# Softmax minus one-hot: stores move to Pool as single DMA packets and wait for a load four rows ahead

## The chip, the core and the metric

The kernel runs on one core of a Trainium2 chip. The core has compute engines that work side by side (VectorE, called DVE in the profile; ScalarE, called ACT; GpSimd, called POOL; TensorE, called PE) and SyncE (SP), which here only issues DMAs. All DMAs of the core, whichever engine issues them, are carried out by the same 16 DMA engines. The metric is the device time of one execution in microseconds; the kernel before was run three times: 1248.03 us in the median, 1247.41 to 1248.87.

## The reference

Input are logits of 8 x 1024 x 8192 float32 and one integer label for each of the 8192 rows. The output is the gradient of softmax cross entropy, as large as the logits:

```python
logits_max = np.max(logits, axis=-1, keepdims=True)
exp_logits = np.exp(logits - logits_max)
softmax = exp_logits / np.sum(exp_logits, axis=-1, keepdims=True)
...
one_hot[batch_idx, seq_idx, labels] = 1.0
return (softmax - one_hot).astype(np.float32)
```

So 268.4 MB are read and 268.4 MB are written, and each element is touched a few times in between.

## The kernel before

The 8192 rows of logits are cut into 32 blocks of 256 rows. In a block, partition p of the 128 holds two neighbouring rows, j = 0 and j = 1. The kernel's unit of work, which it calls a row and numbers t = 0 to 63, is one j of one block: 128 partitions with 8192 float32 each, 32 KB a partition, 4 MB in all. Block b is t = 2b and 2b + 1. The large tile `X` holds three blocks (`SLOTS = 3`), so six rows: all that is loaded, computed on in place and not yet stored has to fit in these six places.

For each row t there are these instructions. VectorE finds the negated maximum (`m<-X`, the tensor reduce). ScalarE computes exp(x + m) in place and sums it (`X<-X,m`). VectorE takes the reciprocal of the sum (`r<-s`). ScalarE scales the row by it (`X<-X,r`). VectorE compares a constant row of column numbers (`iota`, in PSUM) with the label and subtracts the resulting one-hot (`X<-iota,lab,X`). The last row is scaled and subtracted in two halves. Ahead of all that, Pool, TensorE and VectorE prepare the column numbers and turn the labels; this borrows the sixth place of `X`, which is why the load of row 5 waits for `w_iota`.

All instructions are issued by a helper `run` (lines 63 to 74), which gives them their semaphore waits; that is why nearly every instruction has line 68 in the profile, and a wait that stands in front of one has line 67. The order on each engine is the order in which the code is written. On VectorE it is: reciprocal of row t, maximum of row t + 1, subtraction of row t.

Loads are issued by SP (`nc.sync`, `load(b)`), on one DMA queue, which is q1 in the profile. The string `LOADS` says how each block is loaded: "r" as two DMAs, one for each row; "w" as one DMA for both rows, so 64 KB contiguous for a partition. Blocks 0 to 4 and 26 to 31 are "r", blocks 5 to 25 are "w". A load waits until the stores of the same place three blocks earlier have landed (`free`).

Stores are issued by ACT (`nc.scalar`, `store(t)`), one DMA for each row, on another queue, which is q10. The store of row t - 1 is written in ACT's order between the exp and the scaling of row t, so it is issued as soon as row t - 1 is finished and ACT comes to it.

Of the kernel before, what the change touches and what calls it, by code (L numbers as in the profile page):

```python
# [7 lines left out]
P = 128  # L8
G = 2
SLOTS = 3  # L10


LOADS = "rrrrrwwwwwwwwwwwwwwwwwwwwwrrrrrr"
STORES = "rrrrrrrrrrrrrrrrrrrrrrrrrrrrrrrr"


@with_exitstack
def kernel(
    ctx: ExitStack,
    tc: tile.TileContext,  # L20
    logits: bass.AP,
    labels: bass.AP,
    out: bass.AP,
):
    nc = tc.nc
    fp32 = mybir.dt.float32
    i32 = mybir.dt.int32
    i16 = mybir.dt.int16
    Act = mybir.ActivationFunctionType
    Alu = mybir.AluOpType  # L30

    x_nv = logits.flatten_outer_dims()
    o_nv = out.flatten_outer_dims()
    N, V = x_nv.shape
    T = N // P
    B = T // G
    lab_bp = labels.rearrange("a b -> (a b)").rearrange("(b q) -> b q", q=G * P)
    x_b = x_nv.rearrange("(b p j) v -> b p j v", p=P, j=G)
    o_b = o_nv.rearrange("(b p j) v -> b p j v", p=P, j=G)

    const = ctx.enter_context(tc.tile_pool(name="const", bufs=1))
    psum = ctx.enter_context(tc.tile_pool(name="psum", bufs=1, space=bass.MemoryType.PSUM))


    X = const.tile([P, SLOTS, G, V], fp32)
    lab_raw = const.tile([B, G * P], labels.dtype)
    lab_f = const.tile([B, G, P], fp32)
    ident = const.tile([B, B], fp32)
    lab = const.tile([P, G, B], fp32)

    m, s, r = (const.tile([P, T], fp32, name=n) for n in ("m", "s", "r"))

    iota = psum.tile([P, V], i16)
    lab_ps = iota[:].bitcast(fp32)[:, :T].rearrange("p (j b) -> p j b", j=G)

    with tc.tile_critical():  # L56
        sem = tc.alloc_semaphore
        got = [[sem(f"got{i}{q}") for q in range(2)] for i in range(SLOTS)]
        put = [[sem(f"put{i}{q}") for q in range(2)] for i in range(SLOTS)]
        lab_got, dve, act, pe, pool = (sem(n) for n in ("lab_got", "dve", "act", "pe", "pool"))  # L60
        count = {}

        def run(engine, waits, counter, method, **operands):

            waits = list(dict.fromkeys(waits))
            for w in waits[:-1]:
                engine.wait_ge(*w)
            instruction = getattr(engine, method)(**operands)  # L68
            for w in waits[-1:]:
                instruction._wait_ge(*w)  # L70
            step = 16 if method == "dma_start" else 1
            instruction.then_inc(counter, step)
            count[counter.name] = count.get(counter.name, 0) + step
            return counter, count[counter.name]


        w_raw = run(nc.scalar, [], lab_got, "dma_start", out=lab_raw[:], in_=lab_bp)
        w = run(nc.gpsimd, [], pool, "memset", ap=ident[:], constant=0.0)
        w_ident = run(
            nc.gpsimd, [w], pool, "affine_select",  # L80
            out=ident[:], in_=ident[:], compare_op=Alu.not_equal, fill=1.0,
            base=0, pattern=[[-1, B]], channel_multiplier=1,
        )

        made = X[:, SLOTS - 1, G - 1, :].bitcast(i16)[:, :V]
        w_made = run(
            nc.gpsimd, [], pool, "iota", out=made, pattern=[[1, V]], base=0, channel_multiplier=0
        )
        step = mybir.dt.size(labels.dtype) // 4
        lab32 = lab_raw[:].bitcast(i32).rearrange("b (p j s) -> b j p s", j=G, s=step)  # L90
        w_lab = run(nc.vector, [w_raw], dve, "tensor_copy", out=lab_f[:], in_=lab32[:, :, :, 0])
        for j in range(G):
            w = run(
                nc.tensor, [w_ident, w_lab], pe, "transpose",
                out=lab_ps[:, j, :], in_=lab_f[:, j, :], identity=ident[:],
            )
        w_turned = run(nc.vector, [w], dve, "tensor_copy", out=lab[:], in_=lab_ps)
        w_iota = run(
            nc.vector, [w_turned, w_made], dve, "tensor_scalar",
            out=iota[:].bitcast(i32), in0=made.bitcast(i32), scalar1=0, scalar2=None, op0=Alu.bitwise_or,  # L100
        )


        every, rows = slice(0, P), slice(0, G)
        PIECES = {
            "r": [(every, slice(j, j + 1)) for j in range(G)],
            "h": [(slice(i, P, 2), rows) for i in range(2)],
            "w": [(every, rows)],
        }

        def meets(a, b):

            sets = [[set(range(*d.indices(n))) for d, n in zip(p, (P, G))] for p in (a, b)]
            return all(x & y for x, y in zip(*sets))


        loaded, stored, finished = {}, {}, []
        last_made = [((every, slice(G - 1, G)), w_iota)]

        def load(b):  # L120
            loaded[b] = []
            before = stored.get(b - SLOTS, last_made if b == SLOTS - 1 else [])
            for q, piece in enumerate(PIECES[LOADS[b]]):
                ps, js = piece
                free = [w for other, w in before if meets(piece, other)]
                w = run(
                    nc.sync, free, got[b % SLOTS][q], "dma_start",
                    out=X[ps, b % SLOTS, js, :], in_=x_b[b, ps, js, :],
                )
                loaded[b].append((piece, w))  # L130

        def store(t):
            b, j = divmod(t, G)
            stored.setdefault(b, [])
            for q, piece in enumerate(PIECES[STORES[b]]):
                ps, js = piece
                if js.stop != j + 1:
                    continue
                w = run(
                    nc.scalar, [finished[t]], put[b % SLOTS][q], "dma_start",  # L140
                    out=o_b[b, ps, js, :], in_=X[ps, b % SLOTS, js, :],
                )
                stored[b].append((piece, w))


        def row(t):
            return X[:, t // G % SLOTS, t % G, :]

        def row_max(t):
            b, j = divmod(t, G)  # L150
            arrived = [w for piece, w in loaded[b] if meets(piece, (every, slice(j, j + 1)))]
            return run(
                nc.vector, arrived, dve, "tensor_reduce",
                out=m[:, t : t + 1], in_=row(t), axis=mybir.AxisListType.X, op=Alu.max, negate=True,
            )


        load(0)
        w_max = row_max(0)
        for t in range(T):  # L160
            x = row(t)
            label = lab[:, t % G, t // G : t // G + 1]
            w = run(
                nc.scalar, [w_max], act, "activation",
                out=x, in_=x, func=Act.Exp, bias=m[:, t : t + 1], scale=1.0, accum_out=s[:, t : t + 1],
            )
            w_sum = run(nc.vector, [w], dve, "reciprocal", out=r[:, t : t + 1], in_=s[:, t : t + 1])
            if t + 1 < T:
                if (t + 1) % G == 0:
                    load((t + 1) // G)  # L170
                w_max = row_max(t + 1)
            if t > 0:
                store(t - 1)

            n = 1 if t + 1 < T else 2
            cols = [slice(i * V // n, (i + 1) * V // n) for i in range(n)]
            scaled = [
                run(
                    nc.scalar, [w_sum], act, "activation",
                    out=x[:, c], in_=x[:, c], func=Act.Copy, bias=0.0, scale=r[:, t : t + 1],  # L180
                )
                for c in cols
            ]
            for c, w in zip(cols, scaled):
                w = run(
                    nc.vector, [w], dve, "scalar_tensor_tensor",
                    out=x[:, c], in0=iota[:, c], scalar=label, in1=x[:, c],
                    op0=Alu.is_equal, op1=Alu.subtract, reverse1=True,
                )
            finished.append(w)  # L190
        store(T - 1)
        for b in range(B - SLOTS, B):
            for _, w in stored[b]:
                nc.scalar.wait_ge(*w)


# [28 lines left out]
```

## Time and profile before

| | |
|---|---|
| time of the runs, median (lowest to highest) | 1248.03 us (1247.41 to 1248.87) |
| span of the profiled execution | 1245.7 us |
| VectorE busy | 1119.2 us, 90% |
| ScalarE busy | 919.1 us, 74% |
| Pool busy | 7.4 us, 1% |
| DMA packets, bytes, mean rate | 15460, 536.98 MB, 431 GB/s |
| from issue to landing: stores, row loads, block loads (median) | 30.8, 26.6, 33.4 us |

The profiled execution's own time is its span, from the first to the last instruction; the time of a run holds a little more around it, so the median is 2.3 us above the span. The tensor reduce takes 8.68 us a row, the exp 7.12, the scaling 7.12 and the subtraction of the one-hot 8.74. Beside the page, the trace holds a record of each DMA packet (its queue, bytes, begin and duration) and of each landing; a packet here is what one DMA engine moves for one descriptor, for example 32 KB of one partition. In the packet records and everywhere else times are counted from the span's start.

### The profile page before, as it was taken

How to read it: one execution, taken by the hardware profiler on the slowest of the kernel's cores; microseconds unless marked ns; L12 is line 12 of the kernel's file. 1: busy time of each engine (PE TensorE's matmuls, PEld its weight loads, DVE VectorE, ACT ScalarE, POOL GpSimd, SP SyncE). 2: the span in 40 equal slices, each digit the busy share in tenths (PEclk: the TensorE clock that was granted, in tenths of full speed). 3: DMA queues.
4: the chain of work that ended last, by engine and by line, in shares of the span. 5: the costliest groups of instructions: out<-in, count | busy, mean ns of one | idle time of the engine just before them, and what ended most of it. 6: DMA issues, size and time to landing. Idle time of an engine off the chain costs nothing.

```text
span 1245.7 us, 592 instructions
## 1 busy us (share of the span) xinstructions
PE 0.4 (0%) x2; PEld 0.3 (0%) x2; DVE 1119.2 (90%) x196; ACT 919.1 (74%) x194; POOL 7.4 (1%) x7
## 2 busy tenths in 40 slices
PE   0000000000000000000000000000000000000000
PEld 0000000000000000000000000000000000000000
DVE  5999998888988889888998888988889999999893
ACT  3888886778776787767877778777777788887772
POOL 2000000000000000000000000000000000000000
DMA  9999999999999999999999999999999999999998
GB/s 406 417 429 433 438 433 442 437 426 427 430 435 445 439 417 442 426 430 437 432 443 438 420 435 432 430 437 450 420 426 437 436 428 432 437 435 429 432 437 386
DMA packets 15460, 536.98 MB, mean 431 GB/s; under 512 B 1728, under 2 KB 1728, under 8 KB 1760
## 3 DMA queue, kind: packets, MB, share of 16 engines
q1 hardware_dynamic: 6192, 268.44, 50.0%
q10 hardware_dynamic: 9264, 268.51, 49.9%
q14 instruction: 4, 0.03, 0.0%
HBM read 268.50 MB, written 268.44 MB: 431 GB/s over the span
## 4 chain that ended last, share of the span: by engine, by line
DMA 59%; DVE 37%; another core or an unknown queue 2%; ACT 1%; DVEq 0%; issue 0%; PE 0%; SPq 0%; ACTq 0%
DMA X<-in_logits_dram 31%; DMA out_dram<-X 27%; DVE m L68 18%; DVE X L68 18%; ACT X L68 1%; DVE iota L68 0%; DVEq L56 0%; DMA lab_raw<-in_labels_dram 0%; DVE lab_f L68 0%; DVE r L68 0%; PE iota L68 0%; SPq L68 0%; ACTq L68 0%; DVE lab L68 0%
## 5 line engine op out<-in xcount | busy, mean ns | idle before, releaser
L68 DVE TENSOR_REDUCE m<-X 128x1 f32<-128x8192 f32 x64 | 555.2, 8675 | 94.3 <-DMA X<-in_logits_dram 94.3
L68 ACT ACTIVATE X<-X,m 128x8192 f32<-128x8192 f32 x64 | 455.9, 7123 | 188.4 <-DVE m L68 188.4
L68 DVE SCALAR_TENSOR_TENSOR X<-iota,lab,X 128x8192 f32<-128x8192 int16 (+1 forms) x65 | 559.7, 8612 | 4.1 <-ACT X L68 4.1
L68 ACT ACTIVATE X<-X,r 128x8192 f32<-128x8192 f32 (+1 forms) x65 | 456.0, 7017 | 115.9 <-DVE r L68 115.9
L68 DVE RECIPROCAL r<-s 128x1 f32<-128x1 f32 x64 | 9.9, 154 | 7.3 <-ACT X L68 7.3
L68 ACT ACTIVATION_READ_ACCUMULATOR X<-X,m 128x1 f32 x64 | 12.0, 187 | 0.0
L68 DVE CAST lab_f<-lab_raw 32x256 f32<-32x256 int32 x1 | 3.7, 3685 | 4.7 <-DMA lab_raw<-in_labels_dram 4.7
L68 POOL IOTA X<- 128x8192 int16 x1 | 6.9, 6944 | 0.0
L68 DVE TENSOR_SCALAR iota<-X 128x4096 int32<-128x4096 int32 x1 | 4.4, 4427 | 0.1
L68 ACT ACT_TABLE_LOAD x1 | 1.3, 1283 | 1.3 <-SPq L56 1.3
L68 DVE COPY lab<-iota 128x64 f32<-128x64 f32 x1 | 0.2, 225 | 0.5 <-PE iota L68 0.5
L68 PE MATMUL iota<-ident,lab_f 32*128 32x32 f32 x2 | 0.4, 300 | 8.5 <-DVE lab_f L68 8.5
L68 PEld LDWEIGHTS iota<-ident,lab_f 32*128 32x128 f32 x2 | 0.3, 196 | 8.4 <-DVE lab_f L68 8.4
L68 POOL TENSOR_SCALAR_AFFINE_SELECT ident<-ident 32x32 f32<-32x32 f32 x1 | 0.2, 204 | 0.1
L68 POOL MEMSET ident<- 32x32 f32 x1 | 0.1, 115 | 0.5 <-SPq L56 0.5
L209 POOL MEMSET const-bfloat16-1.0<- 128x1 bf16 x1 | 0.1, 107 | 0.0
L209 POOL MEMSET const-uint8-127<- 128x1 uint8 x1 | 0.1, 107 | 0.0
L209 POOL MEMSET const-float32-0.0<- 128x1 f32 x1 | 0.1, 104 | 0.2 <-issue 0.2
L209 POOL MEMSET const-float32-1.0<- 128x1 f32 x1 | 0.1, 104 | 0.0
## 6 DMA issues: line engine op xcount, KB each, us to landing
out_dram<-X ACTq DMA_DIRECT2D x64, 4096.0 KB, 30.8
X<-in_logits_dram SPq DMA_DIRECT2D x22, 4096.0 KB, 26.6
X<-in_logits_dram SPq DMA_DIRECT2D x21, 33.4
lab_raw<-in_labels_dram ACTq DMA_DIRECT2D x1, 64.0 KB, 3.8
```

The costliest lines, as they stand in the source:

```text
L68: instruction = getattr(engine, method)(**operands)
L209: nc = _bacc.Bacc("TRN2", target_bir_lowering=False, num_devices=1)
```

## The change

Loads go row by row for all 64 rows: `load(t)` replaces `load(b)`, the strings `LOADS` and `STORES` and the table `PIECES` go away, and a load of row t waits for the store of row t - 6 alone. Stores are issued by Pool (`nc.gpsimd`) instead of ACT, with `single_packet=True`, which asks for one DMA packet for each engine instead of one for each descriptor; each engine's share of a row's store is 8 partitions, 256 KB. The store of row t additionally waits until the load of row t + 4 has landed (`AHEAD = 4`); the last four stores, and so those of rows 60 to 63, have no such wait of their own. A store is written in Pool's order once the load it waits for has been written. The closing waits for the last six stores are Pool's.

```diff
-LOADS = "rrrrrwwwwwwwwwwwwwwwwwwwwwrrrrrr"
-STORES = "rrrrrrrrrrrrrrrrrrrrrrrrrrrrrrrr"
+AHEAD = 4
...
+        loaded, stored, finished, stores = {}, {}, [], []
+
+        def load(t):
+            b, j = divmod(t, G)
+            free = w_iota if t == SLOTS * G - 1 else stored[t - SLOTS * G] if t >= SLOTS * G else None
+            loaded[t] = run(
+                nc.sync, [free] if free else [], got[b % SLOTS][j], "dma_start",
+                out=X[:, b % SLOTS, j, :], in_=x_b[b, :, j, :],
+            )
 
         def store(t):
             b, j = divmod(t, G)
...
+            ahead = [loaded[t + AHEAD]] if t + AHEAD < T else []
+            stored[t] = run(
+                nc.gpsimd, ahead + [finished[t]], put[b % SLOTS][j], "dma_start",
+                out=o_b[b, :, j, :], in_=X[:, b % SLOTS, j, :], single_packet=True,
+            )
...
-        load(0)
+        for t in range(G):
+            load(t)
         w_max = row_max(0)
         for t in range(T):
             x = row(t)
...
                 if (t + 1) % G == 0:
-                    load((t + 1) // G)
+                    for j in range(G):
+                        load(t + 1 + j)
                 w_max = row_max(t + 1)
             if t > 0:
-                store(t - 1)
+                stores.append(t - 1)
+            while stores and min(stores[0] + AHEAD, T - 1) in loaded:
+                store(stores.pop(0))
...
             finished.append(w)
-        store(T - 1)
-        for b in range(B - SLOTS, B):
-            for _, w in stored[b]:
-                nc.scalar.wait_ge(*w)
+        for t in stores + [T - 1]:
+            store(t)
+        for t in range(T - SLOTS * G, T):
+            nc.gpsimd.wait_ge(*stored[t])
```

## The prediction

> **What bounds the kernel now.** I read four views of the profile, from the whole to the edges. First the page's totals and queues:
>
> ```profile
> span 1245.7 us, 592 instructions
> PE 0.4 (0%) x2; PEld 0.3 (0%) x2; DVE 1119.2 (90%) x196; ACT 919.1 (74%) x194; POOL 7.4 (1%) x7
> ...
> DMA packets 15460, 536.98 MB, mean 431 GB/s; under 512 B 1728, under 2 KB 1728, under 8 KB 1760
> ...
> q1 hardware_dynamic: 6192, 268.44, 50.0%
> q10 hardware_dynamic: 9264, 268.51, 49.9%
> ```
>
> Queue 1 carries the loads (issued by SP), queue 10 the stores (issued by ACT). Together they fill 99.9% of the 16 DMA engines. VectorE at 90% is second. Then the busy time by stretch: loads alone, the first store's arrival, the middle, stores alone.
>
> ```profile
> 13.00:47.00 34.00, 0.00 (x0) 0.00 (x0) 26.72 (x7) 21.55 (x5) 0.00 (x0) 1.00 1.00 432
> 47.00:70.00 23.00, 0.00 (x0) 0.00 (x0) 23.00 (x5) 19.66 (x4) 0.00 (x0) 1.00 1.00 410
> 160.00:960.00 800.00, 0.00 (x0) 0.00 (x0) 716.08 (x124) 592.12 (x124) 0.00 (x0) 1.00 1.00 434
> ...
> 1205.00:1243.00 38.00, 0.00 (x0) 0.00 (x0) 21.05 (x5) 14.83 (x5) 0.00 (x0) 1.00 0.99 427
> ```
>
> The last two columns are the DMA share and GB/s. Reading alone (432), writing alone (427) and the mixture (434) run at the same rate, so sorting reads from writes has no gain to collect here. The packet records say it finer: a packet of 32 KB takes 1.213 us on its engine in all three stretches, load or store, and a 64 KB packet of a whole-block load 2.418. Third, the waits:
>
> ```profile
> ACT X L68 <- DVE m L68: 188.4, 64, 19.7
> ACT X L68 <- DVE r L68: 115.9, 64, 2.1
> DVE m L68 <- DMA X<-in_logits_dram: 94.3, 25, 6.9
> ...
> SPq L68 <- DMA out_dram<-X: 699.1, 37, 57.3
> SPq L67 <- DMA out_dram<-X: 446.9, 21, 21.5
> ```
>
> VectorE, the busiest engine, waits only for loads; the loads' issuer waits nearly always for a store to free a slot. Last the edges, from the order of time:
>
> ```profile
> 0.96 2.12 SPq L68 DMA_DIRECT2D X<-in_logits_dram  x4
> ...
> 46.98 0.36 ACTq L68 DMA_DIRECT2D out_dram<-X  x1
> ...
> 1199.76 8.69 DVE L68 TENSOR_REDUCE m<-X 128x1 f32<-128x8192 f32 x1 [1.93 <-DMA X<-in_logits_dram]
> ...
> 1230.18 0.34 ACTq L68 DMA_DIRECT2D out_dram<-X  x1
> ```
>
> The packet records show the first load packet at 2.15 us and the last store packet ending at 1244.16, so 1242.0 us of DMA. Each engine carries 8 of a row's 128 partitions, one packet each. Loads: 22 row loads x 8 x 1.213 = 213.5 and 21 block loads x 8 x 2.418 = 406.2, together 619.7. Stores: 64 x 8 x 1.213 = 621.1. Sum 1240.8: the engines are never idle, and 1.2 us at most is lost. That loss shows in the 410 GB/s row: when the first store joined, two load packets on each engine were stretched (1.16 us per engine in all). The kernel's time is 2.15 + DMA work + 1.5 of closing. The three runs' median, 1248.03, is 2.3 above the profiled span; I work in differences to the span and add them to the median.
>
> **The change, part by part.**
>
> Loads by rows throughout. 21 block loads become 42 row loads. Two 32 KB packets cost 2 x 1.213 = 2.426 against 2.418, 0.008 more; 21 x 8 x 0.008 = **+1.3 us** on every engine. The 21 additional issues on SP (0.33 each) lie inside SP's waits, 1146 us of them, at nothing; without those waits they would cost 7 us.
>
> One packet per engine for a store. The 0.008 us is what a packet costs beyond its bytes (1.205 per 32 KB, which is 27.2 GB/s per engine). If eight descriptors in one packet pay it once, each store saves 7 x 0.008 = 0.058, and 64 stores save 3.7; if the cost belongs to the descriptor, nothing. No row decides; I take the middle, **-1.8 us**, and keep 0 and -3.7. The Trainium skill, "DMA: Bandwidth & Descriptors", section "Why small descriptors are slow (HBM only)", says the packet's share is about 3 cycles and that the descriptor's own metadata is not amortized by packing; with its 850 MHz this gives an estimate of 64 x 7 x 3.5 ns = 1.6 us saved, which would leave the sum 0.2 higher.
>
> Stores from ACT to Pool. ACT loses 64 issues of 0.34 us. They stand between a reciprocal and the scaling activation, which ACT waits 1.8 us for per row, while VectorE reduces the next row: worth nothing, since both engines wait for loads in the end. At the very end the scaling of row 63 starts 0.4 earlier; its store is queued behind others anyway. Pool has no other work after 8.3 us, so nothing queues behind its waits but later stores, and SP's loads behind those.
>
> The hold: store t waits for load t+4. What is late next? Take a cycle from the moment load t+4's last byte lands. Load t+5 is already queued and runs. Pool sees the landing 0.37 us later (last load: landed 1199.39, VectorE started 1199.76) and needs p until its store's packet is at the engines. The packet then holds each engine for 8 x 1.213 = 9.70. SP sees its end 0.36 later (first store: 71.01, load issued 71.37) and its load reaches the engines 1.2 after the issue (0.96 to 2.15). So load t+6 is there at 0.37 + p + 9.70 + 1.56 = 11.6 + p, while load t+5 keeps the engines busy until 2 x 9.70 = 19.4. There is no gap while **p is under 7.8 us**. Nor does computing become late: row 62 landed at 1180.0 and was finished at 1217.0, 37 us, and the hold gives it four periods of 19.4, 78. VectorE needs 17.3 us a row. A further queue restart per row costs nothing by the nearest row: in the middle stretch the load queue ran dry 21 times for about 10.5 us, and no restart lengthened packets on all engines. The bound on the other side is the first store's 1.16 us (a rival below).
>
> The end. Today stores are queued behind each other when the last load lands, and no gap appears. Under the hold nothing but load 63 is queued in its last microseconds: store 58 ran earlier, store 59 waits for it. So the engines stand idle for 0.37 + p. After that stores 59 to 62 (38.8 us) cover the 30 us that row 63 takes to its store (1199.76 to 1230.18). What is p? The trace has no store of Pool's. From below: SP's cold start, 1.2. From above: the first store on ACT, issued 46.98, first packet recorded 52.18, 5.2 (with loads in between). I take 2.0, nearer the cold start, since the engines are empty at that moment too, with some time for Pool to write descriptors itself. Gap 0.37 + 2.0 = **+2.4 us** (1.6 to 5.6).
>
> Start and closing stay: the first loads, the first store's stall, the last wait (now Pool's) of 1.5.
>
> Sum: +1.3 - 1.8 + 2.4 = +1.9. Span 1247.6, median **1249.9**. Bounds: +1.3 - 3.7 + 1.6 = -0.8 to +1.3 + 0 + 5.6 = +6.9, 1247.2 to 1254.9. Within 0.2% (1245.5 to 1250.5; about what a measurement of this kernel can tell from no change) lies the larger part.
>
> **The rivals.**
>
> A, Pool hands over late (slower). If p exceeds 7.8 us, each further microsecond leaves a gap in nearly every one of some 58 cycles. Pool being made to wait for the VectorE instruction under way (8.6 to 8.7 us) would do it: p spread between 2 and 10.7 exceeds 7.8 a third of the time, by 1.4 on average, 58 x 0.33 x 1.4 = 27, with 4 more at the end: about 1281. In favour: VectorE is 90% busy. Against: its instructions take 8.67 us for 8192 elements, one every 1.06 ns, no doubled rate. The Trainium skill, "SBUF — State Buffer", section "SBUF: two separate sides", states such a lock-out of Pool's descriptor writing, but for VectorE's two-port modes alone, and this trace shows no instruction at such a rate.
>
> B, stores restart badly (slower). The stall of 1.16 us per engine came when the store queue began from empty; afterwards it hardly ever emptied. In the changed kernel it starts from empty at nearly every row. If every start paid that, 64 x 1.16 = 74: 1324. If packets from Pool's queue were only 1% longer, 0.01 x 621 = 6: 1256. Against the first: the load queue's 21 restarts, and two moments (179 and 217 us) when the store queue seems to have been empty for a packet and nothing was stretched. It decides from 0.04 us per store.
>
> C, the packet cost vanishes and the gap is short (faster). Everything at its best: -3.7 + 1.3 + 1.6 = -0.8, and the first store's stall gone because it meets a different moment, -1.2: -2.0, 1246.0; to pass 0.2% something unseen must help as well, for instance packets of a store beginning under the end of a load. About 1245.
>
> D, the flag does nothing: stores still go as eight packets, sharing engines by turns with loads. Then load 63 and store 58 end close together, the gap is covered, and only +1.3 is left: 1249.3.
>
> **How the numbers follow.** My forecast 0.58 (0.40 of it within 0.2%, 0.18 slower), A 0.10, B 0.17, C 0.08, D 0.07. Hence faster 0.08, same 0.47, slower 0.45. The likeliest is the forecast, 1249.9, with its own range 1247.2 to 1254.9. For 8 in 10 the range goes down to 1245 (half of C left out) and up to 1270, which takes in B's mild form and leaves out A's and B's larger prices (0.14).
>
> **What would show it.** Right: Pool's queue with far fewer or single 256 KB store packets, loads at 1.213 us each, VectorE's wait for loads like today's 94 us, the DMA share at 9 in all slices, a dip of 2 to 3 us where the last load lands, store 59 issued there. The store packet's length settles the saving: 9.64 for eight descriptors, or 9.70. Wrong: gaps in every cycle with Pool's issue long after the landing (A); load packets stretched at each store's begin, or stores over 9.70 (B); a rate above 434 GB/s in the middle (C); 32 KB store packets alternating with loads (D).

## The result, and the profile after

The changed kernel takes 1274.92 us in the median (1273.64 to 1278.16, four runs) against 1247.76 for the kernel before (now the median of four runs): a ratio of 1.0222, with a 95% interval of 1.021 to 1.0235. It is 27 us slower; the prediction had said 1249.9 with a range up to 1270. The page of the changed kernel, its totals and queues:

```profile
span 1271.9 us, 652 instructions
PE 0.4 (0%) x2; PEld 0.3 (0%) x2; DVE 1118.9 (88%) x196; ACT 919.0 (72%) x194; POOL 41.7 (3%) x71
...
DMA packets 18485, 536.99 MB, mean 422 GB/s; under 512 B 2064, under 2 KB 2064, under 8 KB 2096
...
q1 hardware_dynamic: 9216, 268.44, 50.4%
q0 software_dynamic: 9216, 268.44, 49.1%
```

The queues still fill 99.5% of the DMA engines, yet the rate fell from 431 to 422 GB/s: the engines are not idle, they are slower. And q0, Pool's store queue, has 9216 packets for 64 stores: 128 of data and 16 of semaphores each. One packet per engine would have been 64 x 32. Since a record stands for one descriptor, the count alone does not settle what an engine treats as one packet; the order of the records, further down, does. The same stretches of time as before:

```profile
13.00:47.00 34.00, 0.00 (x0) 0.00 (x0) 26.72 (x7) 21.55 (x5) 0.00 (x0) 1.00 1.00 432
47.00:70.00 23.00, 0.00 (x0) 0.00 (x0) 23.00 (x5) 19.97 (x4) 1.21 (x2) 1.00 1.00 410
160.00:960.00 800.00, 0.00 (x0) 0.00 (x0) 719.61 (x125) 598.92 (x126) 21.32 (x40) 1.00 1.00 425
1205.00:1243.00 38.00, 0.00 (x0) 0.00 (x0) 34.22 (x8) 28.86 (x7) 2.12 (x4) 1.00 1.00 434
```

Loads alone and the first store's arrival are unchanged (432, 410). The middle lost: 425 GB/s instead of 434, at a DMA share that still reads 1.00. The waits, and of the issuers' own waits the two that matter:

```profile
POOL out_dram L67 <- DMA X<-in_logits_dram: 1151.6, 59, 44.4
ACT X L67 <- DVE m L67: 223.8, 64, 19.7
DVE m L67 <- DMA X<-in_logits_dram: 109.7, 23, 5.6
...
SPq L67 <- DMA out_dram<-X: 1159.7, 58, 58.5
...
SPq L55 <- POOLq L55: 25.7, 1, 25.7
```

The hold binds for 59 of the 60 stores that have it. VectorE waits for loads a little longer (109.7 instead of 94.3). SP's closing wait is now for Pool.

The packet records say where it went. From the first load packet to the last store packet it is 1262.9 us (2.14 to 1265.02) instead of 1242.0: +20.9. From there to the end it is 6.8 us instead of 1.6: +5.3. Together 26.2, the whole difference of the spans. Of the 20.9, 1.3 is the row loads' packet work (1242.1 per engine instead of 1240.8), and 19.8 is packets that take longer than their 1.213 us: this stretching is 22.0 us per engine, 2.2 before. The two come to 21.1; the 0.2 too much lies in short gaps and in the 3 to 4 ns by which the records of packets that follow each other overlap.

They sit in one place. This is one DMA engine's order of 32 KB packets from about 480 us on (L a load's, S a store's, in brackets the time of a stretched one), put together from the packet records by the begin and end of each:

```
changed kernel: L L L L L L L L(1.55) L(1.27) S L S L S L S S S S S S S S S S(1.34) L S L S L S L
```

Stores come in groups of two rows, and between the groups the engine has loads only. When the next group begins, the last two loads ahead of it are stretched, by 0.55 us together on average; where loads return after stores alone, the last store and the first load are stretched by another 0.15 together, most of it on the store. Pool's issues show the pairs:

```profile
486.28 0.53 POOL L67 DMA_DIRECT2D out_dram<-X  x1 [22.92 <-DMA X<-in_logits_dram]
...
502.69 0.53 POOL L67 DMA_DIRECT2D out_dram<-X  x1 [15.87 <-DMA X<-in_logits_dram]
...
525.69 0.53 POOL L67 DMA_DIRECT2D out_dram<-X  x1 [22.47 <-DMA X<-in_logits_dram]
...
542.18 0.53 POOL L67 DMA_DIRECT2D out_dram<-X  x1 [15.96 <-DMA X<-in_logits_dram]
```

They are 16.4 and 23.0 us apart by turns. The store at 502.69 joins while the one before is under way, those at 486 and 525 find the store queue empty.

### The profile page after: what moved, and what is told of

It reads as the page before. It is cut to its first block, busy times and chain, and to the rows that moved or that the text cites. A ratio compares the mean times of both kernels' runs of the same rounds, so it can differ in the third digit from the quotient of the medians.

```text
span 1271.9 us, 652 instructions
## 1 busy us (share of the span) xinstructions
PE 0.4 (0%) x2; PEld 0.3 (0%) x2; DVE 1118.9 (88%) x196; ACT 919.0 (72%) x194; POOL 41.7 (3%) x71
## 3 DMA queue, kind: packets, MB, share of 16 engines
q1 hardware_dynamic: 9216, 268.44, 50.4%
q0 software_dynamic: 9216, 268.44, 49.1%
## 4 chain that ended last, share of the span: by engine, by line
DMA 71%; DVE 25%; issue 1%; ACT 1%; DVEq 0%; POOL 0%; PE 0%; POOLq 0%; ACTq 0%; SPq 0%
DMA X<-in_logits_dram 35%; DMA out_dram<-X 35%; DVE m L67 12%; DVE X L67 12%; ACT X L67 1%; DVE iota L67 0%; DVEq L55 0%; DMA lab_raw<-in_labels_dram 0%; DVE lab_f L67 0%; DVE r L67 0%; POOL out_dram L67 0%; PE iota L67 0%; POOLq L66 0%; DVE lab L67 0%; ACTq L198 0%
## 5 line engine op out<-in xcount | busy, mean ns | idle before, releaser
L67 DVE TENSOR_REDUCE m<-X 128x1 f32<-128x8192 f32 x64 | 555.1, 8673 | 109.7 <-DMA X<-in_logits_dram 109.7
L67 POOL DMA_DIRECT2D out_dram<-X x64 | 34.2, 535 | 1203.3 <-DMA X<-in_logits_dram 1151.6
## 6 DMA issues: line engine op xcount, KB each, us to landing
X<-in_logits_dram SPq DMA_DIRECT2D x64, 4096.0 KB, 19.8
```

## The experiments

Two theories stood at first. "Start": a store that reaches engines holding only loads stretches those loads, whoever issues it, and the hold makes this happen some 30 times. "Pool": it is Pool's queue or its descriptors. The first four runs part them, and look at the flag and the closing.

**The hold without Pool.** Stores go back to ACT's hardware queue, without the flag; each is written two rows later, so that ACT does not stand long in the hold.

```diff
-                nc.gpsimd, ahead + [finished[t]], put[b % SLOTS][j], "dma_start",
-                out=o_b[b, :, j, :], in_=X[:, b % SLOTS, j, :], single_packet=True,
+                nc.scalar, ahead + [finished[t]], put[b % SLOTS][j], "dma_start",
+                out=o_b[b, :, j, :], in_=X[:, b % SLOTS, j, :],
...
-            while stores and min(stores[0] + AHEAD, T - 1) in loaded:
+            while stores and (stores[0] <= t - 3 or t >= T - 2):
...
-            nc.gpsimd.wait_ge(*stored[t])
+            nc.scalar.wait_ge(*stored[t])
```

> The changed kernel with its hold of four rows, but the stores are issued by ACT on its hardware queue (each written two rows later in ACT's order, where the load it waits for is about to be waited for anyway). Theory 'start' (a store that reaches DMA engines holding only loads stretches about two load packets on each engine, some 0.7 to 0.8 us, whoever issues it; the hold makes the store queue run empty, so this happens some 30 times): load packets stretched by about 19 us per engine as in the changed kernel, the closing back at 1.5 us, so about 1268 to 1271. Theory 'Pool' (the descriptors that Pool writes, or its queue, stretch the loads): no stretched loads beyond the first store's, about 1249 to 1250.

Measured: 1287.27 us, ratio 1.0315 (1.03 to 1.033). The windows of this run, an early one and the middle, ACT's wait, and its first store:

```profile
56.00:106.00 50.00, 0.00 (x0) 0.00 (x0) 50.00 (x9) 42.54 (x9) 0.00 (x0) 1.00 0.71 294
160.00:960.00 800.00, 0.00 (x0) 0.00 (x0) 704.34 (x123) 581.57 (x123) 0.00 (x0) 1.00 1.00 425
...
ACT X L67 <- DMA X<-in_logits_dram: 184.5, 29, 7.5
...
73.01 0.37 ACTq L67 DMA_DIRECT2D out_dram<-X  x1
```

The middle runs at the changed kernel's 425 GB/s, with 24.8 us of stretching per engine. So Pool is not needed for it. The time is above the expected 1268 to 1271 for a reason of this version's own: between 56 and 106 us the DMA engines are busy for 0.71 of the time, since the first store, written two rows later in ACT's order, goes out at 73.0 us instead of 52.7, and the next load waits for it. The records show 18.7 us of gaps per engine, most of them there; without them it would be at about 1269 by the sum.

**Pool without the hold.**

```diff
-            ahead = [loaded[t + AHEAD]] if t + AHEAD < T else []
+            ahead = []
...
-            while stores and min(stores[0] + AHEAD, T - 1) in loaded:
+            while stores:
```

> The changed kernel without the hold: Pool still issues the stores with the one-packet flag, each as soon as its row is finished. Theory 'start': the store queue seldom empties, so only a few starts (1 to 3 us in all) are left; with the 1.3 us of row loads and Pool's 5.3 us closing about 1254 to 1257. Theory 'Pool': 64 stores with Pool's descriptors stretch as before, 1270 or more.

Measured: 1253.27 us, ratio 1.0043 (1.0028 to 1.0057). The middle of this run:

```profile
160.00:960.00 800.00, 0.00 (x0) 0.00 (x0) 734.57 (x127) 606.11 (x127) 22.32 (x42) 1.00 1.00 433
```

433 GB/s, and stretching of 1.4 us per engine, most of it (1.1) at the first store. Between the first and the last data packet it takes 1242.2 us, as the kernel before does. The theory "Pool" is out; the hold costs 21.7 us (1274.9 against 1253.3), and the 5.5 left over the kernel before are, within 0.2 us, the 5.3 that the changed kernel and this one take longer behind the last packet.

**Without the flag.** Only `single_packet=True` is taken out.

> The changed kernel without the one-packet flag. In the changed kernel's trace the store packets are still 32 KB of 1.213 us each and alternate one by one with loads, so by the theory that the flag does nothing here: the same time, 1272 to 1278, the same stretched loads. By the rival that the flag makes the stores' first packets crowd out the loads' reads: stretched loads fall well below 19 us per engine, 1260 or less.

Measured: 1275.55 us, ratio 1.0214 (1.0193 to 1.0235), with the same packets and 19.5 us of stretching in the profiled execution (itself the fastest of its four, 1270.9). The flag moved neither the packets nor, by these runs, the time.

**The closing waits on ACT.** The change alone, with `nc.scalar.wait_ge(*stored[t])` at the end. The expectation speaks of a drain: the instruction at the end of each engine's program that waits until the engine's own work is done.

> The changed kernel, only the closing waits for the last six stores stand on ACT instead of Pool. If the 6.9 us between the last store packet and the end (1.5 before) are Pool's drain, which takes 5.3 us and starts only after Pool's last wait: it runs beside the last stores, about 5.3 us less, 1269 to 1270. If Pool's drain lasts until its DMAs are done, no gain: 1275.

Measured: 1273.92 us, ratio 1.0209 (1.0193 to 1.0224): an inconclusive 1 us. In the trace the last store packet to the end is 3.9 us, 2.9 less than in the changed kernel, but this execution had 27.3 us of stretching, so its time does not show it. SP, which closes the program, waits for ACT and then a little for Pool:

```profile
SPq L55 <- ACTq L55: 21.3, 1, 21.3
...
SPq L55 <- POOLq L55: 2.4, 1, 2.4
```

Neither form of the expectation was right: Pool's drain began early, at 1249.7 us, and ended 3.0 us after the last packet, 2.7 after its landing. It waits for Pool's DMAs and then takes a while.

**The dose.** The hold for rows 0 to 29 alone.

```diff
-            ahead = [loaded[t + AHEAD]] if t + AHEAD < T else []
+            ahead = [loaded[t + AHEAD]] if t < 30 else []
...
-            while stores and min(stores[0] + AHEAD, T - 1) in loaded:
+            while stores and (stores[0] >= 30 or stores[0] + AHEAD in loaded):
```

> The changed kernel with the hold for the stores of rows 0 to 29 alone; the later ones go as soon as their row is finished. A test of dose. Theory 'start': about 15 store starts from an empty queue at 0.7 to 0.8 us instead of some 30, so about half of the 20 us that the hold costs (1274.9 with it, 1253.3 without): 1262 to 1266. If the cost were a constant of some other kind (the first holds or the last ones alone): near 1253 or near 1275.

Measured: 1266.75 us (1264.64 to 1268.62), ratio 1.0153 (1.0139 to 1.0167): 13.5 of the 21.7 us, that is 62%, and a little above the expected 1262 to 1266. Within the run, a window under the hold and one behind it:

```profile
160.00:600.00 440.00, 0.00 (x0) 0.00 (x0) 407.00 (x70) 336.46 (x71) 11.69 (x22) 1.00 1.00 426
700.00:1200.00 500.00, 0.00 (x0) 0.00 (x0) 449.14 (x78) 371.31 (x78) 13.81 (x26) 1.00 1.00 433
```

The loss stops where the hold stops.

**A hold of three rows.** Only `AHEAD = 3`.

> The changed kernel with a hold of three rows. Theory 'start': the cost over the run without a hold (1253.3) is the number of store starts from an empty queue times 0.75 us, whatever the hold; a store released one load earlier is issued with the store before it still under way more often, so fewer starts, 1255 to 1268, and the stretched time and the count of starts in the trace must agree. If the hold itself costs per store: 1275 as with four.

Measured: 1253.20 us, ratio 1.0045 (1.0029 to 1.006), no different from no hold and below the expected 1255 to 1268. Yet this hold binds: Pool waits for loads ahead of 55 stores. Its issues, and the middle:

```profile
482.40 0.53 POOL L67 DMA_DIRECT2D out_dram<-X  x1 [18.81 <-DMA X<-in_logits_dram]
501.76 0.53 POOL L67 DMA_DIRECT2D out_dram<-X  x1 [18.83 <-DMA X<-in_logits_dram]
521.10 0.53 POOL L67 DMA_DIRECT2D out_dram<-X  x1 [18.81 <-DMA X<-in_logits_dram]
...
160.00:960.00 800.00, 0.00 (x0) 0.00 (x0) 734.84 (x127) 606.39 (x127) 21.79 (x41) 1.00 1.00 433
```

They come 19.4 us apart, evenly, and each joins a store still under way. One engine's packets over the same time:

```
hold of three:  S L S L S L S L S L S L L S L S S L S L S L S L S L L S L S S L S L S L
```

No long run of either kind, nothing stretched (1.6 us in all). So, in this kernel, waiting does not cost; letting the store queue run empty does.

**A hold of five rows.** With six places no load can then be queued when a store is released; the loads are written one by one for it (`load(len(loaded))` behind each store, six at the start).

> The changed kernel with a hold of five rows instead of four, loads written one by one. With six places no load can be queued when load t + 5 lands, so a store starts on engines with no load in hand and a load on engines with no store. Theory 'start' in its narrow form (what is stretched are load packets in hand when the store arrives): few stretched packets, under 6 us per engine; instead the engines idle in nearly all of some 58 cycles for Pool's hand-over p + 0.4 us and for the load's 1.6 us, which measures p: with p of 2 to 3 us about 4 to 5 us a row, 1480 to 1540. If every change between writing and reading costs the 0.7 us by itself, packets are stretched as well, 58 x 0.7 = 40 us on top.

Measured: 1520.38 us (one run). The middle of it:

```profile
160.00:960.00 800.00, 0.00 (x0) 0.00 (x0) 594.16 (x103) 489.69 (x103) 17.53 (x33) 1.00 0.84 351
```

Here the engines really are idle, for 0.16 of the time. From a load's last packet to the store's first it is 2.3 us on each engine (2.0 from the slowest engine's end), and from a store's last to the load's first 1.6: this is the price of the hand-overs, 59 times. The loads ahead of a store are not stretched at all (0.001 us), as the narrow form said; but the first load packet after each pause is, by 0.56 us, 33 us in all. That is over the 6 us of the narrow form and under the 40 of the other, and the expectation had not named it.

The count across the kernels, per engine; a start is a store packet behind three or more load packets in a row, and stretching is the time of data packets beyond 1.213 (2.418) us, differences under some 0.02 us left out, from one profiled execution each. Which packets follow each other on an engine is put together from their times, so the counts are good to some tenths:

| kernel | store starts | stretching, us | median of the runs, us |
|---|---|---|---|
| before | 1.4 | 2.2 | 1247.8 |
| changed | 30.3 | 22.0 | 1274.9 |
| hold of four on ACT | 31.3 | 24.8 | 1287.3 (18.7 of gaps) |
| Pool, hold of four, no flag | 30.3 | 19.5 | 1275.6 |
| closing on ACT | 30.6 | 27.3 | 1273.9 |
| hold for the first 30 rows | 15.7 | 12.2 | 1266.8 |
| hold of three | 2.1 | 1.6 | 1253.2 |
| no hold | 1.3 | 1.4 | 1253.3 |

The price of a start is not fixed: with 30 starts each, three kernels had 19.5, 22.0 and 27.3 us of stretching, 0.65 to 0.91 us a start. The profiled executions' own times follow it. Less the stretching, the execution without the flag (1270.91 us) comes to 1251.4, that of the changed kernel (1273.64) to 1251.6, the one with the closing on ACT (1275.90, with its 2.9 us of shorter closing added back) to 1251.5, and those of a hold of three and of no hold (1253.13 and 1253.20) to 1251.5 and 1251.8.

**Row loads alone.** The kernel before, with "r" for all 32 blocks in `LOADS`.

> The kernel before with all loads by rows (stores by ACT, no hold): one part of the change alone. By the packet times, 21 x 8 x 0.008 = 1.3 us more work per engine: 1249.3. If the smaller loads keep the two queues better mixed (the run without the hold had 0.8 us less stretching and 0.7 us fewer gaps): 1248, no change.

Measured: 1248.12 us, ratio 1.0004 (0.9995 to 1.0013). The 1.3 us of packet work are there in the records (1242.1 per engine), but 0.5 to 0.7 us less of stretching stand against it. The time is 0.5 us above its own round's 1247.58, and the interval, -0.6 to +1.6, holds both forms of the expectation.

**What is behind the last packet.** Two edits of the run without a hold. First the closing waits on ACT:

> The run without the hold (1253.3), with the closing waits on ACT instead of Pool: the closing measured where nothing else varies. With the hold, the same edit moved Pool's drain so that it ended 3.0 us after the last store packet, instead of starting after the last wait and taking 5.3; there the median hid it. Theory 'Pool's drain outlasts its DMAs by about 3 us': 1253.3 - 2.9 = 1250.4. If the drain's 5.3 us follow the last landing anyway: 1253.3; if nothing but Pool's own wait caused it: 1248.

Measured: 1250.42 us in the median of nine (1250.1 to 1257.7), ratio 1.0031 (1.0018 to 1.0043), as expected: 2.9 us less. Then the store of row 63 by ACT as well, on a semaphore of its own:

```diff
-                nc.gpsimd, ahead + [finished[t]], put[b % SLOTS][j], "dma_start",
+                nc.scalar if t == T - 1 else nc.gpsimd, ahead + [finished[t]], last if t == T - 1 else put[b % SLOTS][j], "dma_start",
...
-            nc.gpsimd.wait_ge(*stored[t])
+            nc.scalar.wait_ge(*stored[t])
```

> The same, and the store of row 63 alone is issued by ACT. Pool's last store is then row 62's, which lands about 10 us earlier, so Pool's drain is over before the last landing: the closing should be the 1.5 us of the kernel before, 1247.6 to 1248.3, which would leave nothing of Pool's part of the change in the time. If Pool's stores cost something more than the closing (hand-over, descriptors), it stays above 1249.

Measured: 1248.00 us in the median of eleven (1247.5 to 1251.6), ratio 1.0006 (0.9997 to 1.0015). SP's closing wait names Pool no more:

```profile
SPq L55 <- ACTq L55: 14.9, 1, 14.9
```

With 63 of 64 stores on Pool the kernel is as fast as before. All that Pool costs here is its closing, and that only when one of its DMAs is the last. No version beat the kernel before, and the reason is in the prediction's first view: the DMA engines were busy throughout.

## Why the prediction was wrong

The forecast was +1.9 us on three terms; measured are +27. Two of the signs that it had listed under "wrong" came together: load packets stretched where stores begin (B), and 32 KB store packets alternating with loads (D). By its own steps:

- **"A further queue restart per row costs nothing by the nearest row"**: this is the step that failed. The row chosen was that of the load queue's 21 restarts; the row that applied was the other one the prediction named and priced, the first store's 1.16 us. Rival B has the mechanism, a store queue that starts from empty, and the trace of before had exactly one clean case of it. Its price of 74 us was too high on both factors: 30 starts instead of 64, because the releases come in pairs, and 0.55 us with 0.15 for the returning loads instead of 1.16. 30 x 0.7 = 21, against a measured cost of the hold of 21.7.
- **The cycle and its 7.8 us**: it assumed that a store holds its engine for 9.70 us. The packets alternate one by one instead, so stores and loads run side by side until the loads are through. No gap appeared in the middle, as the step said, but not by its reasoning. Its parts were sized well: 0.37 + p was put at 2.4 and was 2.0 in the run with a hold of five (2.3 on each engine by itself), and SP's 1.56 was 1.6 on each engine (1.3 from the slowest engine's end). Rival A, Pool held up by VectorE, did not occur: Pool's issues take 0.53 us each, and in the run with a hold of five, where VectorE nearly always began its 8.69 us maximum as the load landed (53 waits), the store's first packet came 1.9 to 3.0 us behind the load's last on every engine. The Trainium skill, "SBUF — State Buffer", section "SBUF: two separate sides", limits the lock-out to VectorE's two-port modes, and the trace agrees so far as it goes: no instruction here ran at a doubled rate, and none held Pool up.
- **"One packet per engine", -1.8 us**: nothing. Rival D was right on this: store packets stay at 32 KB and 1.213 us, and stores and loads alternate by single packets. (The prediction's bound of -3.7 holds a slip: 7 x 0.008 is 0.056, which gives 3.6; nothing hangs on it.) The Trainium skill, "DMA: Bandwidth & Descriptors", section "Queues, rings and completion order", says that an engine drains a whole packet of typically 9 to 17 descriptors before it turns to another queue. In these runs an engine turned after a single descriptor's 32 KB, with the flag and without it; by that rule, had the flag made one packet of a store's eight descriptors, the engine would have stayed with them.
- **The gap at the end, +2.4 us**: none. It rested on store 58 being through before load 63; sharing the engines, it was not (no gap over 1 us in the changed kernel's records), as D had it.
- **"Start and closing stay"**: the closing grew by 5.3 us. The prediction moved the last waits to Pool without asking what Pool does after its last wait: a drain of 5.3 us that begins behind that wait. In the kernel before, ACT's drain after the same waits took 0.01 us.
- **Row loads, +1.3 us**: right in the packets; the time alone can't tell (+0.5, with an interval of -0.6 to +1.6).

The three foreseen terms came to +1.3 instead of +1.9. That they agree so nearly is luck, since two of the three did not occur and had opposite signs. The time came from two costs booked at zero, 21.7 us for the hold and 5.3 for the closing.

## What to carry to other kernels

In a kernel whose DMA engines are always busy, look at single packets: a share of 1.00 does not say that each packet goes at its speed. Mix reads and writes evenly; in this kernel a wait that let the store queue run dry cost 0.7 us at each new start, while a milder wait (three rows instead of four here) cost nothing. When work moves to another engine, follow that engine's instructions to the program's end, its drain too, and leave the last DMA to an engine whose closing is short.

## What the runs showed of the hardware that was not expected

- A store that arrives at engines with only loads in hand stretches the two load packets ahead of it, by 0.55 us together on average in the changed kernel, and by 1.16 at the first store of the kernel before; stores issued by ACT and by Pool do so alike. Why the reads slow down is open: no run looked inside a packet. Open too is why returning loads cost 0.15 us here and 0.02 in the kernel before, where they came as 64 KB packets.
- A load that starts on idle engines has a first packet longer by 0.56 us; a store on idle engines does not (both in the run with a hold of five).
- Pool's stores run at the same 1.213 us per 32 KB as the hardware queues' and reach the engines 2.0 us after the last packet of the load they wait for, where nothing else is queued (hold of five). Pool's drain at the program's end ends 2.7 us after the last landing of its DMAs if it was already waiting (3.0 after the last packet in the run with the closing on ACT), and takes 5.3 us if it begins after it.
